# First stage of a streaming encoder step: other PSUM tiles for the first products and the token sums

## The chip, the cores and the metric

One core of a Trainium2 chip runs the whole program. The metric is the device time of one execution in microseconds (us); of several runs the median is given. The engines are PE (TensorE; PEld is its weight load), DVE (VectorE), ACT (ScalarE), POOL (GpSimd) and SP (SyncE, which here only issues DMAs).

## The reference, cut to what matters

One trunk layer is computed for 1024 prompt tokens and 32 sample tokens, with D = 1024. Only its beginning matters here: an RMS normalisation whose scale and shift come from a small matrix product with the condition `c`, and then one wide input projection, of which the first column blocks are keys, values and queries of the attention.

```
mod = silu(c) @ w_ada + b_ada
sh1, sc1, ... = split(mod)
h = rmsnorm(x, g_mix) * (1 + sc1) + sh1
u = h @ w_in
qa, ka, va, qm, km, vm, om, ip, fp, ga, gm = split(u)
# then: chunk-band attention on qa, ka, va; an mLSTM on qm..fp; merge gates ga, gm;
# output projection and residual; SwiGLU FFN and residual; final RMSNorm
```

## The kernel before

The 1024 + 32 tokens stand in the free dimension, in three token tiles of 352 columns (`TILES`); the first two are called early, the third late. The 1024 model channels stand in eight groups of 128 partitions (`k` = 0 to 7). Every product is made in three passes (`PASSES`), since weights and activations are each split into a high and a low part: high weight with high activation, low weight with high activation, high weight with low activation. A projection block is 128 columns of `w_in`; one block over one token tile takes 8 x 3 = 24 matmuls of 128x352.

`first_units` is the first stage. It makes the scales and shifts (`ada_sums` on PE, `ada_done` on ACT), the sums of squares of each token (`token_sums` on PE, read by DVE in `token_roots`), and then the products of three blocks at once: K, V and Q of the first pair of heads. For the two early tiles it goes through `k` = 0 to 7 and makes six matmuls in each pass (`products`); meanwhile ACT, DVE and POOL make the next `h` (`scaled_x`, `high_h`, `low_h`). At `k` = 3 PE makes the token sums of the late tile, POOL takes the roots, and at `k` = 4 PE spreads them (transposes on L543) and ACT copies them out (L544). `late_h` then makes the late tile's `h`. After the early products ACT and DVE take their results out of PSUM (`put_k`, `put_v`, `put_q`, lines 601 to 606, 642, 702 to 706). PE's next work is the late tile of K and V: 48 matmuls of line 475, `k` by `k`, K and V in turn, into the two places called `last`. The late tile of Q follows as an ordinary `unit` (line 402), into whose run the transposes of V (`v_tail`, L674; its results are taken out by ACT L662 and DVE L665) and of its sample rows (`v_sample`, L623 and L625) are put. Then come the next projection blocks, and with the second head pair's blocks the attention of the first (scores in a tile of `ps_s`, transposes in `ps_t`, values in `ps_v`).

PSUM has eight banks here: three tiles of one bank (`mm`), one tile `psS` of two banks, one tile `psT` of two banks (called `psA` in `first_units`), one tile `psV` of one bank (called `psH`). `tok` is the second half of a tile of two banks.

The order of the instructions of PE, ACT, DVE and POOL is the order of the code (`manual_schedule`); each of these engines works through its own list in that order. The waits between engines are put in by the framework, from which instruction writes or reads which tile.

## Time and profile before

| | |
|---|---|
| median of 3 runs | 1601.08 us (1599.99 to 1601.38) |
| the profiled execution | 1600.62 us, of which its span 1598.9 us |
| PE busy | 1569.6 us, 98% of the span |
| DVE, ACT, POOL busy | 1104.7, 793.8, 418.0 us |
| mean granted TensorE clock | 0.996 |

The span runs from the first to the last instruction of the profiled execution; 1.7 us of its time lie outside. Times in the views below are us from the start of the span. Matmuls overlap: one of 352 columns is listed with some 0.32 us, while the next starts 0.16 us after it. In a list of waits the engine that waited stands on the left and what it waited for on the right of the arrow. Tile names come without their numbers, and `s` stands for many tiles.

### The profile page before, as it was taken

The page shows a single profiled execution, that of the slowest core. Times are in us where ns is not written, and L with a number is a line of the kernel's source. Part 1 is how long each engine was busy: PE and PEld are TensorE (multiplying, and loading weights), DVE is VectorE, ACT ScalarE, POOL GpSimd, SP SyncE. Part 2 cuts the span into 40 slices and gives each one's busy share as a digit, 9 for nine tenths or more (in the row PEclk, how much of TensorE's full clock was granted, in tenths as well). Part 3 has the DMA queues.
Part 4 walks back from the last instruction along what each step waited for, and adds up shares of the span by engine and source line. Part 5 has one row for each costly group of instructions (what it writes and reads, how often), then busy time and mean ns, then how long its engine had stood idle before and what let it go on. Part 6 is the DMA issues. An engine that isn't in the chain of part 4 may idle for free.

```text
span 1598.9 us, 27295 instructions
## 1 busy us (share of the span) xinstructions
PE 1569.6 (98%) x10197; PEld 1552.4 (97%) x10197; DVE 1104.7 (69%) x2276; ACT 793.8 (50%) x1748; POOL 418.0 (26%) x439
## 2 busy tenths in 40 slices
PE   8899999999999999999999999999999999999997
PEld 8889999999999999999999999999999999999997
DVE  3656565556676845456654699988898886799755
ACT  4666454544555644444443655554544444545443
POOL 0324233433232411000012100566565650000000
PEclk9999999999999999999999999999999999999999
DMA  9222323242232332575353311313222227427444
GB/s 375 84 65 84 107 76 116 82 130 93 67 87 74 83 90 75 121 259 187 122 153 114 107 55 44 103 54 107 81 78 96 67 77 249 145 80 240 138 136 155
DMA packets 176329, 186.02 MB, mean 116 GB/s; under 512 B 11746, under 2 KB 141446, under 8 KB 176198
## 3 DMA queue, kind: packets, MB, share of 16 engines
q1 hardware_dynamic: 173542, 182.45, 36.1%
q10 hardware_dynamic: 2656, 1.83, 0.4%
q8 instruction: 80, 1.31, 0.3%
q14 instruction: 51, 0.42, 0.1%
HBM read 150.10 MB, written 34.16 MB: 115 GB/s over the span
## 4 chain that ended last, share of the span: by engine, by line
PE 90%; ACT 4%; DVE 3%; DMA 2%; issue 1%; POOL 0%; ACTq 0%; SPq 0%; DVEq 0%; POOLq 0%
PE mm L402 40%; PE psb L1869 18%; PE mm L1869 10%; PE psb L2251 3%; PE mm L946 3%; PE mm L2251 2%; PE psV L851 2%; PE psb L2115 2%; PE psS L792 1%; PE psT L819 1%; PE mm L2115 1%; DMA s<-in_w_ada_dram 1%; DMA s<-in_x_dram 1%; PE psV L1180 1%; PE psT L1182 1%
## 5 line engine op out<-in xcount | busy, mean ns | idle before, releaser
L402 PE MATMUL mm<-s,wsp 128*128 128x352 f32 x4104 | 687.0, 324 | 0.0
L402 PEld LDWEIGHTS mm<-s,wsp 128*128 128x128 f32 x4104 | 657.3, 188 | 1.8 <-issue 0.4
L365 DVE TENSOR_TENSOR wsp<-wraw,wsp 128x512 fp32r<-128x512 f32 (+1 forms) x280 | 235.9, 860 | 118.7 <-ACT wsp L364 116.7
L1869 PE MATMUL psb<-s,wsp 128*128 128x352 f32 x1611 | 271.7, 322 | 1.6 <-DVE wsp L365 0.9
L364 ACT ACTIVATE wsp<-wraw 128x512 fp32r<-128x512 f32 x336 | 199.6, 617 | 143.9 <-PE psb L1869 43.0
L1869 PEld LDWEIGHTS psb<-s,wsp 128*128 128x128 f32 x1611 | 260.6, 188 | 2.1 <-DVE wsp L365 1.1
L1869 PE MATMUL mm<-s,wsp 128*128 128x352 f32 x933 | 159.3, 322 | 0.0
L1869 PEld LDWEIGHTS mm<-s,wsp 128*128 128x128 f32 x933 | 151.2, 188 | 0.4 <-DVE wsp L365 0.4
L812 POOL TENSOR_SCALAR st<-st,mx 128x640 f32<-128x640 f32 (+5 forms) x72 | 53.2, 739 | 187.1 <-DVE mx L811 165.0
L1275 DVE CUSTOM_DVE_ANT_0 junk<-wa,t 128x512 bf16<-128x512 f32 x128 | 93.6, 731 | 1.1
L365 POOL TENSOR_TENSOR wsp<-wraw,wsp 128x512 fp32r<-128x512 f32 x56 | 74.7, 1354 | 56.8 <-ACT wsp L364 50.5
L806 DVE CUSTOM_DVE_ANT_0 st<-psS,bias 128x640 f32<-128x640 f32 (+5 forms) x72 | 44.5, 617 | 57.3 <-PE psS L792 42.5
L807 ACT ACTIVATE st<-st,mx 128x640 f32<-128x640 f32 (+5 forms) x72 | 47.9, 666 | 63.5 <-DVE mx L806 62.4
L1816 POOL TENSOR_TENSOR t<-t,sl 128x352 f32<-128x352 f32 x19 | 18.4, 968 | 212.7 <-ACT sl L1814 212.7
L826 ACT ACTIVATE pT<-psT 128x640 fp32r<-128x640 f32 (+3 forms) x80 | 38.5, 492 | 61.8 <-PE psT L819 49.3
L2224 POOL TENSOR_TENSOR fst<-fst,mhalf 128x6 f32<-128x6 f32 x1 | 2.3, 2311 | 221.1 <-DVE fst L2223 221.1
L831 DVE TENSOR_TENSOR pT<-psT,pT 128x640 fp32r<-128x640 f32 (+3 forms) x80 | 44.0, 558 | 22.5 <-ACT pT L826 22.4
L1488 POOL TENSOR_TENSOR wraw<-wraw,raw 128x512 f32<-128x512 f32 x33 | 55.8, 1704 | 0.9
L946 PE MATMUL mm<-s,s 128*128 128x264 f32 (+3 forms) x432 | 54.5, 283 | 0.0
L2251 PE MATMUL psb<-s,wsp 128*128 128x352 f32 x330 | 54.2, 324 | 0.0
L2251 PEld LDWEIGHTS psb<-s,wsp 128*128 128x128 f32 x330 | 53.1, 188 | 0.1
L946 PEld LDWEIGHTS mm<-s,s 128*128 128x128 f32 (+1 forms) x432 | 51.9, 179 | 0.5
(377 smaller groups left out, 2480.1 us busy)
## 6 DMA issues: line engine op xcount, KB each, us to landing
wraw<-in_w_in_dram SPq DMA_DIRECT2D x37, 512.0 KB, 3.6
wraw<-in_w_gate_up_dram SPq DMA_DIRECT2D x33, 512.0 KB, 4.0
wa<-in_w_mod_dram SPq DMA_DIRECT2D x64, 256.0 KB, 2.6
wraw<-in_w_down_dram SPq DMA_DIRECT2D x32, 512.0 KB, 4.5
a_d<-t SPq DMA_DIRECT2D x22, 528.0 KB, 2.6
g_d<-t SPq DMA_DIRECT2D x16, 528.0 KB, 3.0
t<-g_d SPq DMA_DIRECT2D x16, 528.0 KB, 4.6
s<-in_w_ada_dram SPq DMA_DIRECT2D x16, 512.0 KB, 8.6
```

The lines of the kernel that those rows point to most:

```text
L364: act.activation(dst[:, 0], src, AF.Copy)
L365: eng.tensor_tensor(dst[:, 1], src, f(dst[:, 0]), op=ALU.subtract)
L402: pe.matmul(pt[:, :hi - lo], wt[(w0 + k) // 4][:, a, (w0 + k) % 4], xt[k][:, b, lo:hi], start=(k == 0 and q == 0), stop=(k == n - 1 and q ...
L806: dve.tensor_tensor_reduce(so, sv, bi, -1.0, 3.0e38, ALU.add, ALU.min, mx[:n, 1:2])
L807: act.activation(st[:n, :w], st[:n, :w], AF.Exp, bias=mx[:n, 1:2], scale=-1.0, accum_out=mx[:n, 2:3])
L812: pool.tensor_scalar(st[:n, :w], st[:n, :w], mx[:n, 3:4], 1.0, op0=ALU.mult, op1=ALU.mult)
L946: pe.matmul(pt[:n, :wd], hs[k][:, a, i * P:i * P + n], whl[b][:, k, :wd], start=(k == 0 and q == 0), stop=(k == KD - 1 and q == 2))
L1275: dve.tensor_tensor_reduce(junk, wa, crow[:, c], 1.0, 0.0, ALU.mult, ALU.add, at)
L1488: self.eng.tensor_tensor(a(dst), a(x), a(y), op=op)
L1869: pe.matmul(acc, wt[:, a, k], x[k][:, b], start=(start and not onto and k == 0 and q == 0), stop=(stop and k == 3 and q == 2), skip_group_ ...
L2115: pe.matmul(acc, wt[k // 4][:, u, k % 4], piece_of[k, i][:, v], start=(k == 0 and q == 0), stop=(k == KP - 1 and q == 2))
L2251: pe.matmul(acc, wt[(k - k0) // 4][:, u, (k - k0) % 4], piece_of[k, 2][:, v], start=(k == 0 and q == 0), stop=(k == NF - 1 and q == 2))
```

## The change

It gives other tiles to the same instructions; no instruction is added, removed or moved. The token sums go from the second half of `psA` to that of `psS`; the sums for channel group 7 from `psH` to the first half of `psS`. V's two early tiles go from `psS` to `psA`, Q's from the first half of `psA` and an `mm` tile to an `mm` tile and `psH`. The late tiles of K and V go from `tok` (in `psA`) and `psH` to the two halves of `psS`.

```
-    tok = psA[:, 512:]
+    tok = psS[:, 512:]
...
-        pts = [[mmt(), mmt()], [psS[:, :512], psS[:, 512:]], [psA[:, :512], mmt()]]
-        last = [tok, psH]
+        pts = [[mmt(), mmt()], [psA[:, :512], psA[:, 512:]], [mmt(), psH]]
+        last = [psS[:, :512], tok]
...
-        ada_sums(7, 0, psH)
-        ada_sums(7, 1, psH)
+        ada_sums(7, 0, psS)
+        ada_sums(7, 1, psS)
...
-        ada_done(7, psH)
+        ada_done(7, psS)
```

The waits that the framework puts in change with the tiles. In the rows below `mm_363` and `mm_364` hold K, `s_347` to `s_550` are `h` of `k` = 0 to 7, and a wait names the engine waited for.

PE at `k` = 3, the token sums of the late tile and the third pass behind them, before:

```order
L304 MATMUL psT_150<-ones,t_153 128x32 [waits DVE_49]
L304 MATMUL psT_150<-ones,t_153 128x32
L304 MATMUL psT_150<-ones,t_153 96x32
L475 MATMUL mm_363<-s_422,wsp_327 128x352
L475 MATMUL mm_364<-s_422,wsp_327 128x352
L475 MATMUL psS_152<-s_422,wsp_330 128x352 x2
L475 MATMUL psT_150<-s_422,s_345 128x352 [waits DVE_49]
L475 MATMUL mm_365<-s_422,s_345 128x352
```

and after:

```order
L304 MATMUL psS_152<-ones,t_153 128x32 [waits DVE_49]
L304 MATMUL psS_152<-ones,t_153 128x32
L304 MATMUL psS_152<-ones,t_153 96x32
L475 MATMUL mm_363<-s_422,wsp_327 128x352
L475 MATMUL mm_364<-s_422,wsp_327 128x352
L475 MATMUL psT_150<-s_422,wsp_330 128x352 x2
L475 MATMUL mm_365<-s_422,s_345 128x352
L475 MATMUL psV_151<-s_422,s_345 128x352
```

The matmul of Q behind the sums waited for DVE, which reads the sums in the other half of its tile; it now has no wait.

PE where the early products end and the late tile of K and V begins, before (Q's early results are in `psT_150` and `mm_365`):

```order
L475 MATMUL psT_150<-s_550,s_345 128x352
L475 MATMUL mm_365<-s_550,s_345 128x352
L475 MATMUL psT_150<-s_347,wsp_327 128x352 [waits Activation_49]
L475 MATMUL psV_151<-s_347,wsp_330 128x352
L475 MATMUL psT_150<-s_347,wsp_327 128x352
L475 MATMUL psV_151<-s_347,wsp_330 128x352
L475 MATMUL psT_150<-s_347,wsp_327 128x352 [waits Pool_49]
L475 MATMUL psV_151<-s_347,wsp_330 128x352
L475 MATMUL psT_150<-s_390,wsp_327 128x352
```

and after:

```order
L475 MATMUL mm_365<-s_550,s_345 128x352
L475 MATMUL psV_151<-s_550,s_345 128x352
L475 MATMUL psS_152<-s_347,wsp_327 128x352 [waits Activation_49]
L475 MATMUL psS_152<-s_347,wsp_330 128x352
L475 MATMUL psS_152<-s_347,wsp_327 128x352
L475 MATMUL psS_152<-s_347,wsp_330 128x352
L475 MATMUL psS_152<-s_347,wsp_327 128x352 [waits Pool_49]
L475 MATMUL psS_152<-s_347,wsp_330 128x352
L475 MATMUL psS_152<-s_390,wsp_327 128x352 [waits Activation_49]
```

K and V of the late tile now stand in one tile, and each `k` has a wait for ACT of its own, where one wait on the first matmul covered all of them.

ACT where the late tiles of K and V are taken out (L601 and L604 read K, L642 reads V), before:

```order
L364 ACTIVATE wsp_741<-wraw_497 128x512 [waits PE_49]
L601 ACTIVATE s_657<-psT_150 64x352 [waits PE_49]
L601 ACTIVATE s_657<-psT_150 64x352
L604 ACTIVATE kf_658<-psT_150 128x352
L642 ACTIVATE t_668<-psV_151 128x352 [waits PE_49]
L662 ACTIVATE s_766<-mm_767 128x8x64 [waits PE_49]
```

and after:

```order
L364 ACTIVATE wsp_741<-wraw_497 128x512 [waits PE_49]
L601 ACTIVATE s_657<-psS_152 64x352 [waits PE_49]
L601 ACTIVATE s_657<-psS_152 64x352
L604 ACTIVATE kf_658<-psS_152 128x352
L642 ACTIVATE t_668<-psS_152 128x352 [waits DVE_49]
L662 ACTIVATE s_766<-mm_767 128x8x64 [waits PE_49]
```

ACT's read of V's late tile now waits for DVE, whose two reads of K's late tile (L606) are in the same tile.

## The prediction

> **What bounds the kernel now.** I read the page's first and fourth part, then the chain of waits in order of time, then PE's own waits from 24 to 84 us, and last the timeline around each of them.

> ```profile
> PE 1569.6 (98%) x10197; PEld 1552.4 (97%) x10197; DVE 1104.7 (69%) x2276; ACT 793.8 (50%) x1748; POOL 418.0 (26%) x439
> PE 90%; ACT 4%; DVE 3%; DMA 2%; issue 1%; POOL 0%; ACTq 0%; SPq 0%; DVEq 0%; POOLq 0%
> ```

> PE is busy nearly throughout and carries 90% of the chain that ended last, so a microsecond in which PE stands still in the first stage is, as far as this goes, a microsecond of the whole. PE's waits in the stage that the change touches are these:

> ```profile
> PE psT L475 <- ACT s L704: 3.7, 1, 3.7
> PE psT L475 <- DVE roots L315: 1.1, 1, 1.1
> ```

> Both are matmuls on `psT`, held up by a reader of the same tile's other contents. The longer one stands between the early products and the late tile:

> ```profile
> 64.40 1.86 ACT L601 ACTIVATE s<-mm 64x352 fp32r<-64x352 f32 x4
> 64.48 0.32 PE L475 MATMUL mm<-s,s 128*128 128x352 f32 x1
> 64.57 0.25 POOL L356 TENSOR_TENSOR s<-s,s 128x32 fp32r<-128x32 f32 x1 [0.77 <-ACT s L348]
> 67.53 0.95 ACT L704 ACTIVATE s<-psT 64x352 fp32r<-64x352 f32 x2
> 68.53 0.66 PE L475 MATMUL psT<-s,wsp 128*128 128x352 f32 x1 [3.73 <-ACT s L704]
> 68.86 0.93 ACT L704 ACTIVATE s<-mm 64x352 fp32r<-64x352 f32 x2
> 78.84 1.61 PE L402 MATMUL mm<-s,s 128*128 128x352 f32 x9
> ```

> PE starts its last early product at 64.48 and stands until ACT has taken Q out of `psT` (67.53 + 0.95). And it comes back slow, as the granted clock (the number behind POOL's in each row) and the chain show:

> ```profile
> 67.00:68.00 1.00, 0.00 (x0) 0.00 (x0) 0.68 (x2) 0.99 (x3) 0.00 (x0) 0.63 0.00 0
> 68.00:74.00 6.00, 5.47 (x19) 5.47 (x20) 2.57 (x4) 1.72 (x4) 2.72 (x4) 0.50 0.00 0
> 74.00:75.00 1.00, 1.00 (x8) 1.00 (x8) 0.00 (x0) 0.00 (x0) 0.00 (x0) 0.96 0.00 0
> 73.68 0.49 PE L475 MATMUL psV<-s,wsp 128*128 128x352 f32 x1
> 73.59 0.29 PE psT L475
> 77.56 0.16 PE psV L475
> ```

> A mean of 0.63 between 67 and 68 means full speed for 0.26 us and half after it: the clock fell at 67.26 and came back at 74.08 (0.96 in the last row: half for 0.08 us). Matmuls follow each other at 0.29 us in that time, at 0.16 outside it.

> **The change, part by part.** All sums are against the profiled execution, 1600.62 us with 1598.9 of span; the median of the runs, 1601.08, lies 0.46 above it.

> *The late tile of K and V.* With no wait the next matmul would start at 64.48 + 0.16 = 64.64. The wait for Q goes, because `psS` holds nothing but token sums and scales by then, both read before 56 us. What is left to wait for is `h` of the late tile: its last piece is POOL's row at 64.57, done at 64.82, and it belongs to `k` = 7, some 7 us later in PE's list; the waits for ACT at each `k` are for that same `h`. So 48 matmuls take 48 x 0.16 = 7.68 us, where before PE needed 78.84 - 64.64 = 14.20 (3.89 of standing, 10.31 of work, of which 2.63 is the half clock). Gain 6.52 us. Between bounds: 3.89 if the clock fell all the same, 6.52 if not; nothing is left that would make PE stand, so I take the upper one.

> *The token sums at `k` = 3 and the spread roots at `k` = 4.*

> ```profile
> 50.62 0.49 PE L475 MATMUL psS<-s,wsp 128*128 128x352 f32 x2
> 52.00 0.15 DVE L315 TENSOR_SCALAR roots<-psT 96x1 f32<-96x1 f32 x1
> 52.20 0.43 PE L475 MATMUL psT<-s,s 128*128 128x352 f32 x1 [1.09 <-DVE roots L315]
> 52.23 1.49 POOL L316 TENSOR_TENSOR roots<-roots,mhalf 128x3 f32<-128x3 f32 x1 [19.27 <-DVE roots L315]
> 52.47 0.33 PE L475 MATMUL mm<-s,s 128*128 128x352 f32 x1
> 54.54 0.47 PE L543 MATMUL psT<-ident,roots 128*128 128x128 f32 x3
> 55.04 0.47 ACT L544 ACTIVATE t<-psT 128x352 f32<-128x352 f32 x1 [1.12 <-PE psT L543]
> 55.19 0.49 PE L475 MATMUL psS<-s,wsp 128*128 128x352 f32 x2
> 55.56 0.43 PE L475 MATMUL psT<-s,s 128*128 128x352 f32 x1
> 55.83 0.32 PE L475 MATMUL mm<-s,s 128*128 128x352 f32 x1
> ```

> Without the wait, the matmul at 52.20 would start at 50.62 + 2 x 0.16 = 50.94 and the one at 52.47 at 51.10: 1.37 us. But DVE's reads stay where they are (DVE works without a break there), and so does POOL's power, done at 53.72, which the transposes need. PE would come to them at 54.54 - 1.37 = 53.17 and now waits: 53.72, 0.05 for the signal (52.15 to 52.20 at the first wait) and some 0.16 for the weight load ahead of it (an estimate: the spacing of two matmuls) give 53.93. So 0.61 of the 1.37 is left, and the new stop is POOL. Then the wait for ACT's copy goes: the matmul at 55.83 would have started at 55.19 + 3 x 0.16 = 55.67, so 0.16 more. Gain 0.77; bounds 0.16 (POOL's end later than listed) and 1.53.

> *ACT's new wait.* K's and V's late results are now one tile. Before, L642 read V beside DVE's reads of K:

> ```profile
> 80.17 0.46 ACT L642 ACTIVATE t<-psV 128x352 f32<-128x352 f32 x1
> 80.31 1.06 DVE L606 TENSOR_TENSOR s<-psT,s 64x352 fp32r<-64x352 f32 x2 [9.61 <-ACT kf L604]
> 80.92 0.60 ACT L662 ACTIVATE s<-mm 128x512 fp32r<-128x512 f32 x1 [0.28 <-PE mm L674]
> 81.68 0.60 PE L674 MATMUL mm<-ident,t 128*128 128x128 f32 x4
> 82.32 0.60 ACT L662 ACTIVATE s<-mm 128x512 fp32r<-128x512 f32 x1 [0.80 <-PE mm L674]
> 82.95 0.69 DVE L665 TENSOR_TENSOR s<-mm,s 128x512 fp32r<-128x512 f32 x1 [0.64 <-ACT s L662]
> 83.55 0.27 DVE L625 COPY stg<-mm 32x128 f32<-32x128 f32 x1
> 83.88 0.59 PE L402 MATMUL mm<-s,wsp 128*128 128x352 f32 x2
> ```

> In these times, L642 moves from 80.17 to 81.37 + 0.05 = 81.42 and ends at 81.88. Queued behind it on ACT are both L662, then a copy with its DMA and Q's L702. The second of the four transposes at 81.68 is the first that reads V's late columns, so PE stands about 0.3 us there; the second L662 goes from 82.32 to about 82.65; DVE's L665 and L625 follow it, and PE's next block waits for L625 at 83.88 already. Cost 0.35; bounds 0 (if ACT need not wait) and 1.25 (all that L642 moves). I take 0.35, by the row of L662, which has 0.80 of idle ahead of it to give.

> *What moves for nothing.* The split of the next weights (ACT L364, POOL L365) now comes before PE's end of the late tile, not in the middle of it:

> ```profile
> 68.08 2.96 POOL L706 TENSOR_SCALAR s<-s 64x352 fp32r<-64x352 f32 x4 [1.23 <-ACT s L704]
> 75.03 1.15 ACT L364 ACTIVATE wsp<-wraw 128x512 fp32r<-128x512 f32 x2 [5.24 <-PE psT L475]
> 75.80 2.54 POOL L365 TENSOR_TENSOR wsp<-wraw,wsp 128x512 fp32r<-128x512 f32 x2 [4.76 <-issue]
> 89.75 0.33 PE L792 MATMUL psS<-s,s 128*128 128x128 f32 x2
> 93.43 0.50 PE L792 MATMUL psS<-s,s 128*128 128x256 f32 x2 [1.35 <-DVE mx L806]
> ```

> ACT is free of Q at 68.86 + 0.93 = 69.79 and splits until 70.94; POOL is free at 71.04 and ends at 73.6. PE uses these weights at 83.88 - 7.29 + 0.35 = 76.94: 3.3 us of cover, and if it went, PE would stand for what POOL is late. The attention's first scores (89.75) need `psS` back, now from V's late read (about 74.6 on the new clock) and not from V's early one; they come at 82.8, so 8 us cover that. PE's wait at 93.43 ends a chain that starts from Q's late tile, which moves along; I leave it as it is.

> **Sum:** 6.52 + 0.77 - 0.35 = 6.94 us. 1600.62 - 6.94 = 1593.68 for an execution like the profiled one, 1594.14 from the median; I say 1594.0.

> **The rivals.** Clear of noise is about 0.2%, 3.2 us.

> *The half clock was not in every run (or comes again elsewhere).* PE stood 3.73 us, the clock fell 2.46 us after the last matmul's listed end at 64.80. If this is near an edge, most runs before may have kept the full clock; then only 6.94 - 2.63 = 4.31 us are won, 1596.8. Against it: the three timed runs lie between 1599.99 and 1601.38 around the profiled 1600.62, and none is 2.6 us below it. 0.07. [...]

> *The gain is given back later.* Something paced by other engines (the wait at 93.43, the chain's 4% of ACT and 3% of DVE) could hold its time while PE comes earlier. For it to eat 4 of 6.9 us, a chain would have to be fixed in time, not in the order; DMA, which alone is, has 2% of the chain. 1599, within 0.2%. 0.04.

> *The change does not do what it says:* the first late matmul's wait for ACT could still be for Q's copies. Against it: each later `k` has a wait for ACT of its own, and those instructions stand ahead of Q's copies in ACT's list, so the first wait is earlier still. About 0.8 - 0.35 would be left, 1600.6. 0.02.

> *Two blocks in turn in one tile.* If PE had to let each matmul land before the next one writes the tile's other half, the 48 would follow each other at the 0.32 us that one is listed with: 7.7 us more, 1601.4. If the gaps let the clock fall too, it is the 0.49 of the row at 73.68: 48 x 0.33 = 15.8 more, 1609.5. It is slower by over 0.2% from 0.16 + (6.94 + 3.2) / 48 = 0.37 us apiece on. Against it: the row at 50.62 has two matmuls into the two halves of `psS` in 0.49 us, which is 0.16 apart. 0.03.

> **How the numbers follow.** My forecast holds 0.84. Its own bounds are 1600.62 - (6.52 + 1.53 - 0) = 1592.6 and, with 0.16 for the token sums and 1.25 for ACT's wait, 1601.08 - 5.43 = 1595.7. The range goes a little past both, for the run-to-run 0.7 us, and up to the first rival's edge: 1592.3 to 1596.8. Faster holds the forecast and the first rival, 0.91; within 0.2% 0.06; slower 0.03.

> **What would show it.** In the new profile PE's waits for ACT L704 and DVE L315 are gone; the granted clock is 1.00 from 62 to 78 us; PE's first L402 starts near 71.5; PE stands some 0.7 us at L543 for POOL; ACT's L642 waits about 1 us for DVE L606; the first L792 comes near 82.8 and everything behind it some 6.9 us earlier, up to a span near 1592. If L402 starts late, the first term is wrong; if it starts at 71.5 and the span does not follow, the cover of a later stage was gone.

## The result, and the profile after

| | before | after |
|---|---|---|
| median | 1601.2 us | 1596.86 us (10 runs, 1596.02 to 1598.06) |
| ratio, 95% interval | | 0.9973 [0.9963, 0.9983] |
| the profiled execution | 1600.62 us | 1598.06 us, its span 1596.3 |
| mean granted clock in it | 0.996 | 0.997 |

The change gains 4.3 us where 6.94 were forecast; the median lies 2.9 us above the forecast and just past the upper end of its range. The profiled execution is the slowest of the ten. Its first loads come later as well: the matmul listed at 35.95 us in the trace of before stands at 36.71, which the following comparisons take off where they say so. Three slow runs of some thousand us (5479.48 of before, 5848.70 of e1, 6770.47 of after_again) are left out of all ranges and ratios; the medians hold them, and would be at most 0.24 us lower without.

The page's busy times and the shares of the chain:

```profile
PE 1568.8 (98%) x10197; PEld 1551.1 (97%) x10197; DVE 1105.4 (69%) x2276; ACT 796.2 (50%) x1748; POOL 421.4 (26%) x439
PE 88%; ACT 3%; DVE 3%; DMA 3%; issue 2%; POOL 0%; SPq 0%; ACTq 0%; DVEq 0%; POOLq 0%
```

PE's waits from 24 to 125 us (what waited, for what, us in total, times, longest):

```profile
PE mm L674 <- ACT t L642: 1.8, 1, 1.8
PE psV L851 <- ACT pT L826: 1.7, 1, 1.7
PE psS L792 <- DVE mx L806: 1.4, 1, 1.4
...
PE psS L543 <- POOL roots L316: 0.5, 1, 0.5
```

PE's waits for ACT L704 and DVE L315 are gone. At L543 the forecast stop for POOL is there. At the head stands a wait that the prediction had put at about 0.3 us. The timeline of PE around the late tile of K and V, and then of ACT and DVE behind it:

```profile
54.58 0.52 PE L543 MATMUL psS<-ident,roots 128*128 128x128 f32 x3 [0.45 <-POOL roots L316]
64.59 7.84 PE L475 MATMUL psS<-s,wsp 128*128 128x352 f32 x48
72.27 1.61 PE L402 MATMUL mm<-s,s 128*128 128x352 f32 x9
75.11 0.27 PE L674 MATMUL mm<-ident,t 128*128 128x128 f32 x1
77.16 0.55 PE L674 MATMUL mm<-ident,t 128*128 128x128 f32 x3 [1.78 <-ACT t L642]
79.31 6.02 PE L402 MATMUL mm<-s,wsp 128*128 128x352 f32 x36
```

```profile
67.49 1.87 ACT L601 ACTIVATE s<-mm 64x352 fp32r<-64x352 f32 x4
72.93 1.16 ACT L364 ACTIVATE wsp<-wraw 128x512 fp32r<-128x512 f32 x2
74.11 0.93 ACT L601 ACTIVATE s<-psS 64x352 fp32r<-64x352 f32 x2
75.55 1.06 DVE L606 TENSOR_TENSOR s<-psS,s 64x352 fp32r<-64x352 f32 x2 [1.73 <-ACT kf L604]
76.64 0.47 ACT L642 ACTIVATE t<-psS 128x352 f32<-128x352 f32 x1 [1.12 <-DVE s L606]
```

All 48 matmuls run through at full speed in 7.68 us (64.59 to 72.27; the row's 7.84 goes to the listed end of the last), and the first L402 comes at 72.27 instead of 78.84. But ACT takes K's early tiles out from 67.49 on (64.40 before), comes to K's late tile at 74.11, 1.8 us after PE has gone on to L402, and V's read, L642, follows at 76.64. PE's second set of transposes has waited 1.78 us for it. So one question is why ACT is 3.1 us later than before, 2.3 beside the start.

A second loss stands further on. The table by stretches (us; PE, PEld, DVE, ACT and POOL busy; granted clock; DMA share; GB/s):

```profile
101.00:104.00 3.00, 1.63 (x11) 1.10 (x9) 1.06 (x3) 2.94 (x5) 0.42 (x1) 1.00 0.20 81
104.00:105.00 1.00, 0.33 (x1) 0.36 (x2) 0.97 (x3) 0.60 (x2) 0.39 (x1) 0.85 0.00 0
105.00:108.00 3.00, 3.00 (x12) 3.00 (x12) 1.65 (x6) 0.92 (x2) 0.80 (x1) 0.50 0.00 0
108.00:109.00 1.00, 1.00 (x7) 1.00 (x7) 0.00 (x0) 0.22 (x1) 0.00 (x1) 0.95 0.00 0
```

Around the stop at L851 the clock fell from 104.70 to 108.11. PE's lead over the trace of before shrinks by 1.54 us there: at L851 it is 109.21 - 104.67 = 4.54 us, at the next L819 112.54 - 109.54 = 3.00.

### The profile page after: what moved, and what is told of

Read it like the earlier page. It is cut to its first block, busy times and chain, and to the rows that moved or that the text cites. A ratio compares the mean times of both kernels' runs of the same rounds, so it can differ in the third digit from the quotient of the medians.

```text
span 1596.3 us, 27296 instructions
## 1 busy us (share of the span) xinstructions
PE 1568.8 (98%) x10197; PEld 1551.1 (97%) x10197; DVE 1105.4 (69%) x2276; ACT 796.2 (50%) x1748; POOL 421.4 (26%) x439
## 4 chain that ended last, share of the span: by engine, by line
PE 88%; ACT 3%; DVE 3%; DMA 3%; issue 2%; POOL 0%; SPq 0%; ACTq 0%; DVEq 0%; POOLq 0%
PE mm L402 38%; PE psb L1869 18%; PE mm L1869 11%; PE psb L2251 3%; PE mm L946 3%; PE mm L2251 2%; PE psV L851 2%; PE psb L2115 2%; PE psS L792 1%; PE psT L819 1%; PE mm L2115 1%; DMA s<-in_w_ada_dram 1%; DMA s<-in_x_dram 1%; PE psV L1180 1%; PE psT L1182 1%
## 5 line engine op out<-in xcount | busy, mean ns | idle before, releaser
L402 PE MATMUL mm<-s,wsp 128*128 128x352 f32 x4104 | 688.6, 324 | 0.1
L402 PEld LDWEIGHTS mm<-s,wsp 128*128 128x128 f32 x4104 | 658.7, 189 | 2.2 <-issue 0.4
L365 DVE TENSOR_TENSOR wsp<-wraw,wsp 128x512 fp32r<-128x512 f32 (+1 forms) x280 | 236.8, 863 | 118.5 <-ACT wsp L364 115.7
L364 ACT ACTIVATE wsp<-wraw 128x512 fp32r<-128x512 f32 x336 | 200.0, 618 | 139.0 <-PE psb L1869 41.5
L365 POOL TENSOR_TENSOR wsp<-wraw,wsp 128x512 fp32r<-128x512 f32 x56 | 74.1, 1344 | 52.0 <-ACT wsp L364 50.5
L806 DVE CUSTOM_DVE_ANT_0 st<-psS,bias 128x640 f32<-128x640 f32 (+5 forms) x72 | 44.5, 618 | 58.7 <-PE psS L792 44.0
L826 ACT ACTIVATE pT<-psT 128x640 fp32r<-128x640 f32 (+3 forms) x80 | 38.6, 494 | 61.6 <-PE psT L819 49.1
```

What stands on the lines that cost most here:

```text
L364: act.activation(dst[:, 0], src, AF.Copy)
L365: eng.tensor_tensor(dst[:, 1], src, f(dst[:, 0]), op=ALU.subtract)
L402: pe.matmul(pt[:, :hi - lo], wt[(w0 + k) // 4][:, a, (w0 + k) % 4], xt[k][:, b, lo:hi], start=(k == 0 and q == 0), stop=(k == n - 1 and q ...
L806: dve.tensor_tensor_reduce(so, sv, bi, -1.0, 3.0e38, ALU.add, ALU.min, mx[:n, 1:2])
```

## Why ACT is late: what the two traces say

POOL makes the late tile's sample columns at L337, right after ACT's L544. The timelines of POOL and ACT, before:

```profile
55.58 1.18 POOL L337 TENSOR_TENSOR s<-s,t 128x32 f32<-128x32 f32 x3 [1.87 <-ACT t L544]
56.69 0.40 ACT L347 ACTIVATE s<-s,sh,s 128x32 f32<-128x32 f32 x1
```

and after:

```profile
55.68 4.44 POOL L337 TENSOR_TENSOR s<-s,t 128x32 f32<-128x32 f32 x3 [1.15 <-ACT t L544]
59.73 0.42 ACT L347 ACTIVATE s<-s,sh,s 128x32 f32<-128x32 f32 x1 [2.26 <-POOL s L337]
```

Three operations on 128x32 took 1.18 us before and 4.44 after, the first alone 4.02. DVE in the same stretch, after:

```profile
55.46 0.95 DVE L354 SCALAR_TENSOR_TENSOR s<-s,sh,s 128x704 fp32r<-128x704 f32 x1
56.32 1.48 DVE L335 SCALAR_TENSOR_TENSOR s<-s,s,t 128x320 f32<-128x320 f32 x3
57.71 1.41 DVE L354 SCALAR_TENSOR_TENSOR s<-s,sh,s 128x320 fp32r<-128x320 f32 x2
59.03 0.55 DVE L335 SCALAR_TENSOR_TENSOR s<-s,s,t 128x320 f32<-128x320 f32 x1
60.90 0.55 DVE L354 SCALAR_TENSOR_TENSOR s<-s,sh,s 128x320 fp32r<-128x320 f32 x1 [1.32 <-ACT s L345]
```

DVE ran L335 and L354 without a break until 59.58, and POOL's first operation ended at 59.70. ACT waited 2.26 us for POOL.

My theory at this point was that the earlier roots bring POOL to its turn inside DVE's stream, where it is kept out, and that this costs PE 1.8 us, with 1.4 more from the clock. The rival was that ACT's new wait behind DVE L606 is simply dearer than I had said.

## The experiments

Each edit stands against the changed kernel. Runs of one job share a chip and its runs of the kernel before; those had medians of 1601.57 (e1 to e4), 1601.03 (after_again, e5 to e7) and 1601.33 us (the rest).

**e1: V's late tile is taken out ahead of K's.**

```
-        W.advance()
+        W.advance(); put_v(*late, last[1][:, :NT]); first[id(W.blocks[1])] = [None] * 3
```

> The changed kernel with V's late tile taken out before K's, so that ACT's L642 has no wait for DVE's L606. Theory 1 (ACT's new wait, met by an ACT that is late already, costs 1.78 us of PE at L674): L642 comes right behind the weight split, near 73.0 + 1.1 = 74.1 us, and ends before V's second transposes want it at 75.2; PE's wait for L642 falls from 1.78 to under 0.3 us; 1.4 to 1.8 us faster than the changed kernel. Rival (the lateness of ACT decides, not its order): K's copies, now behind L642, and the two L662 behind them hold PE as long at the next block (L402 behind L625): under 0.5 us.

1596.54 us (1594.0 to 1597.22), 0.9964 [0.9953, 0.9976]. In its profile PE's second set of transposes has no gap:

```profile
75.00 0.60 PE L674 MATMUL mm<-ident,t 128*128 128x128 f32 x4
```

I first read this as V's order having cured the wait. It could not tell: in this execution POOL's first L337 took 0.84 us, not 4.02, so ACT was not late at all. The clock fell at 424.87 instead, behind another stop, which the kernel had before as well (PE's waits from 410 to 432 us):

```profile
PE psT L819 <- DVE pT L831: 2.0, 1, 2.0
```

This execution took 1596.06 us; what the other runs of e1 met is not seen.

**e2: the sample columns of L337 are made on DVE.**

```
-                pool.tensor_tensor(x, x, RB[:, a:b], op=ALU.mult)
+                dve.tensor_tensor(x, x, RB[:, a:b], op=ALU.mult)
```

> The changed kernel with the late tile's 32 sample columns multiplied by DVE in place of POOL (eight operations of 128x32, L337). Theory 2 (POOL's first L337 took 4.02 us, where it took 0.25 before, because DVE ran on without a gap from 55.5 to 59.6 us; ACT's late h waited 2.26 us for it): ACT's first L347 comes near 57.4 in place of 59.73, ACT ends the copies of Q some 2.3 us earlier and is ready when PE ends the late tile; PE's wait for L642 falls from 1.78 to about 0.3 us, as in the prediction; 1.3 to 1.7 us faster than the changed kernel. Rival (ACT is late for another reason, for example its own reads of PSUM beside a running PE): ACT's L601 for K's early tile stays near 67.5 and the time stays within 0.4 us.

1596.22 us (1594.69 to 1596.48), 0.9966 [0.9953, 0.9978]. The wait for L642 went, but the next POOL operation was shut out, longer still (POOL's timeline):

```profile
57.94 7.50 POOL L356 TENSOR_TENSOR s<-s,s 128x32 fp32r<-128x32 f32 x1 [3.58 <-ACT s L348]
```

DVE went on with its L335, L337 and L354 until 65.3. PE had to wait 0.27 us for that operation inside the late tile. And the clock fell at 425.29. The median gains 0.6 us on the changed kernel's first one, not the 1.3 to 1.7 that I expected.

**e3: the late tile's first L335 goes one place earlier on DVE, so that DVE itself waits for L544 there.**

```
-            if 0 <= k < KD:
+            if 1 <= k < KD:
                 scaled_x(k, *late)
...
-                scaled_x(k + 2, 0, CUT)
+                scaled_x(k + 2, 0, CUT); k == 5 and scaled_x(0, *late)
```

> The changed kernel with one DVE operation moved: the first late L335, which has to wait for ACT's L544, stands one place earlier, ahead of an L354, so that DVE stands still for a moment when POOL's first L337 asks. Same operations on the same engines. Theory 2 in its narrow form (POOL gets in only where DVE has a gap): POOL's first three L337 take about 1.2 us together, as before the change, not 4.44, and the gain is that of the kernel with the sample columns on DVE, 1.3 to 1.7 us. Rival (the sum of DVE's work decides, not the gap): the first L337 still takes over 2 us and the time stays within 0.4 us.

1594.66 us (1594.34 to 1594.95), 0.9958 [0.9945, 0.997]: 6.9 us below before, what the prediction had summed (the repeat further down gives 5.8). POOL gets in at once: the first L337 takes 0.25 us, as before the change, though DVE's L335, which the same L544 released, had started 0.04 us ahead of it. And PE's transposes have no stop of note (timelines of POOL and PE):

```profile
55.83 1.58 POOL L337 TENSOR_TENSOR s<-s,t 128x32 f32<-128x32 f32 x3 [1.15 <-ACT t L544]
75.26 0.95 PE L674 MATMUL mm<-ident,t 128*128 128x128 f32 x4
```

**e4: ACT's side work before the attention starts four steps earlier,** to take the stop at L851 away.

```
-            ada = side.start(ada_rest(), ADA_STEPS, 495)
+            ada = side.start(ada_rest(), ADA_STEPS, 495); [side.step(ada) for _ in range(4)]
```

> The changed kernel with the first Silu of the condition rows (ACT L1269) some 18 us earlier, before the first Exp, which saves ACT two table loads of 1.28 us near 98 and 101 us and so the stall of PE at 103 us (1.73 us, L851 waiting for L826). Theory 3 (this stall lets PE's clock fall for one window of 3.41 us in about half of the executions, which costs 1.4 us there, and splits the runs into 1596.1 and 1597.4): the profile has no half clock between 95 and 115 us, all timed runs lie in one group with the higher mean clock, and the time is 1.5 to 3 us below the changed kernel's. Rival (the clock falls there at random, whatever PE does): the runs still fall into two groups 1.3 us apart.

1595.49 us (1593.78 to 1595.84), 0.996 [0.9946, 0.9974]. The stop did not go away, it moved (PE's waits):

```profile
PE psS L792 <- DVE mx L806: 2.5, 1, 2.5
PE mm L674 <- ACT t L642: 1.7, 1, 1.7
...
PE psV L851 <- ACT pT L826: 0.2, 1, 0.2
```

There is no half clock between 95 and 115 us, as expected, but it now fell behind L792, at 89.54. The median is 1.4 us below the changed kernel's first, where I expected 1.5 to 3. POOL was kept out in this execution (4.44 us for the first three L337), and the wait for L642 stands beside it. The edit also shortened the stop at L819 near 424 us, from 2.0 to 0.84 us, which I had not foreseen.

**after_again and after_third: the changed kernel itself, two more times.**

> The changed kernel once more. Theory 3 (PE's clock falls for 3.41 us at the end of a clock window in which PE stood over about 1.9 us; where the windows lie is another in each execution): in the trace the clock's edges have another phase than before (104.70 and 108.11 us there), and a fall comes only after a window with 2.0 us or more of standing PE; runs between 1596.0 and 1598.1. Theory 2: POOL's first L337 takes 4 us again and PE waits 1.8 us for L642. Rival (both were chance of one execution): POOL's first L337 takes 0.25 us, no wait for L642.

> The changed kernel once more, unedited, to count. Theory (two lots, each drawn anew in every execution): POOL's first operation at L337 takes either about 0.84 us or about 4.0 us, and the granted clock falls for one window of 3.41 us or not. The four levels are then about 1594.2 (neither), 1595.6 (the clock alone), 1596.1 (POOL alone) and 1597.5 us (both), and the runs stand on them; in the profile PE waits 1.5 us or more for ACT L642 if L337 took over 3 us, and under 0.3 us if it took under 1 us. Rival (ACT's new wait for DVE costs this much by itself): PE waits 1.5 us or more for L642 in the profile, however long L337 takes.

Medians of 1597.47 us (eight runs from 1594.16 to 1598.73), 0.9975 [0.9965, 0.9986], and 1595.84 (5 runs, 1594.27 to 1596.45), 0.9964 [0.9952, 0.9977]. Both profiles show an execution some 4 us shorter than the first, with no more than the forecast 0.3 us at L642 and no fall of the clock. The timelines of POOL and ACT, then of PE, in the one of 1594.16 us:

```profile
55.40 1.77 POOL L337 TENSOR_TENSOR s<-s,t 128x32 f32<-128x32 f32 x3 [1.15 <-ACT t L544]
57.09 0.40 ACT L347 ACTIVATE s<-s,sh,s 128x32 f32<-128x32 f32 x1
64.80 1.87 ACT L601 ACTIVATE s<-mm 64x352 fp32r<-64x352 f32 x4
72.22 0.93 ACT L601 ACTIVATE s<-psS 64x352 fp32r<-64x352 f32 x2 [0.84 <-PE psS L475]
74.76 0.46 ACT L642 ACTIVATE t<-psS 128x352 f32<-128x352 f32 x1 [1.13 <-DVE s L606]
```

```profile
72.03 1.61 PE L402 MATMUL mm<-s,s 128*128 128x352 f32 x9
74.87 0.95 PE L674 MATMUL mm<-ident,t 128*128 128x128 f32 x4
77.42 6.05 PE L402 MATMUL mm<-s,wsp 128*128 128x352 f32 x36
```

and the same stretch as above by the clock:

```profile
101.00:104.00 3.00, 1.26 (x10) 1.29 (x10) 2.41 (x8) 1.64 (x6) 0.80 (x1) 1.00 0.00 0
105.00:108.00 3.00, 3.00 (x23) 2.98 (x22) 0.57 (x2) 1.17 (x2) 0.80 (x1) 1.00 0.00 0
```

ACT waits for PE at L601 here, not PE for ACT. L642 waits for DVE just as long (1.13 and 1.12 us), so that wait is not what differs: the rival falls. The stop at L851 is the same too, and the clock stays.

So one kernel has two lots in it, two things that fall out anew in each execution: whether POOL is kept out, and whether the clock falls. Between the two traces of it, PE's L674 differs by 77.16 - 75.27 = 1.89 us, of which 72.27 - 72.03 = 0.24 was there before: being kept out costs 1.65. The clock's fall adds 1.54: the first trace is 104.67 - 102.74 = 1.93 us behind the other at L851 and 109.54 - 106.07 = 3.47 us at the next L819. The clock has a second place to fall, the stop of 2.00 us at L819 near 424 us; it did so in the profiles of e1, e2 and e8. The 23 runs of the changed kernel stand in groups: four at 1594.2 to 1594.7, nine at 1595.8 to 1596.5, nine at 1597.3 to 1598.1 and one at 1598.73. That fits neither, one, both, and one fall more; only the three profiled ones (1594.16, 1594.27 and 1598.06) are seen, so the rest is a reading.

**e5: the part with the token sums alone.** The late tile of K and V waits for Q's place again.

```
-        last = [psS[:, :512], tok]
+        last = [pts[2][0], psS[:, :512]]
```

> The changed kernel, but the late tile of K goes into Q's first mm tile, so that PE waits again until ACT has taken Q out: the token sums' part of the change alone. The prediction's sum for this part: 0.77 us faster than before, 1600.4 to 1600.8. Theory 2 (the earlier copy L544 meets DVE in mid-stream, POOL's L337 takes 4 us, ACT's late h and with it Q's copies end some 2.3 us later): PE stands until near 71.6 us instead of 68.5 and the kernel is slower than before, by 1.5 to 3 us, 1603 to 1604.5.

1602.21 us (11 runs), 1.0009 [1.0, 1.0018]: seven runs at 1600.5 to 1602.3 and four at 1603.4 to 1603.9. The profiled one, the slowest, is of the upper group, and POOL was kept out in it, which PE's wait for Q shows in full (POOL's timeline, then PE's waits):

```profile
55.72 4.44 POOL L337 TENSOR_TENSOR s<-s,t 128x32 f32<-128x32 f32 x3 [1.15 <-ACT t L544]
```

```profile
PE mm L475 <- ACT s L704: 6.8, 1, 6.8
```

**e8: e5 with e3's edit.**

> Token sums and roots in their new tiles, the late tile of K and V still in the old ones (as in e5), and the first late L335 one place earlier on DVE (as in e3). Theory (the token part is worth 0.7 us, and e5 lost it since POOL was kept out at L337): L337 takes under 1 us, PE comes back at L475 within 0.5 us of before and not 3.1 later, about 1600.4 us, the runs within 1.5 us of each other. Rival (the token part costs time by itself, through the later chain of ACT): about 1602.2 us, like e5.

1601.85 us (11 runs, 1600.76 to 1602.24), 1.0003 [0.9994, 1.0012]. The same two views:

```profile
56.02 1.58 POOL L337 TENSOR_TENSOR s<-s,t 128x32 f32<-128x32 f32 x3 [1.15 <-ACT t L544]
```

```profile
PE mm L475 <- ACT s L704: 4.4, 1, 4.4
```

The upper group is gone: no run over 1602.24. But the gain of 0.7 us that I expected is not there. PE's wait for Q has grown from 3.7 to 4.4 us; its end is set by ACT's reads of Q, which come hardly earlier. Beside the start of each trace PE comes to this wait 0.83 us ahead of before and leaves it 0.16 ahead, so most of the token part is lost in it. The first L402 is 1.12 us ahead, since the clock was halved for one window of 3.41 us here and for two before, and another fall at 431.33, behind L819, takes more than that back. So the token part alone shows no gain in the medians, and where POOL is kept out (e5's profile) PE leaves the wait 2.3 us later than before, beside the start. I had e5 and e8 apart by 1.8 us; their medians are 0.4 apart, since only four of e5's eleven runs stand in its upper group.

**e6 and e7: e3 with e1, and with e1 and e4.**

> The kernel with one DVE operation moved (POOL gets its gap) and V taken out before K (no wait of L642 for DVE). With ACT on time, L642's wait is worth what the prediction said, 0.35 us: 1594.3, 0.2 to 0.5 us below the kernel with the gap alone (1594.66), about what can be told. Rival (the wait is worth 1.8 us wherever ACT stands): 1592.9.

> All three: DVE's gap for POOL, V before K, and the early Silu that spares two table loads. Theory 3: PE's wait at L851 near 103 us falls from 1.7 to 0.2 us, that at L792 near 88 us grows by up to 1.1 us since ACT does the Silu ahead of it; 0.5 to 1.5 us below the kernel without the Silu edit, near 1593.2, if no window takes 2 us of standing at L792, and 1.4 more in executions where one does. Rival (table loads were hidden): no difference.

> e3 once more, unedited. Theory (the moved L335 takes away POOL's lot): L337 takes under 1 us, no wait of PE for L642 of 0.3 us or more, 1594.3 to 1595.0 us, a run with the clock's fall up to 1596.0, none above. Rival (e3's five runs were luck of the same draw): runs at 1596.1 and 1597.5 us among them, as in the changed kernel.

> e7 once more, beside e3 on the same chip. Theory: 1593.2 to 1593.9 us, some 1 us below e3, since PE's stop at L851 goes from 1.7 to 0.2 us and the one at L792 grows from 1.4 to 2.5 us, where the clock falls for a window in some executions. Rival (it differs from e3 by the clock's draw alone): the two medians within 0.3 us.

e6: 1595.83 us (1593.88 to 1596.96), 0.9965 [0.9952, 0.9978], 1.5 above what I expected; the second L674 group takes 0.60 us as in e1, and the clock fell at L851, at 103.40. e3 again: 1595.57 us (1594.21 to 1596.58), 0.9964 [0.9951, 0.9976], with two runs above the 1596.0 that I had set as the most. Its profiled run, of 1594.21, has no fall and POOL in at once, so the clock is likely in the other three, but not seen. e7: 1593.65 us (1593.17 to 1593.82), 0.9954 [0.9941, 0.9967], and again 1593.49 (1593.25 to 1593.63), 0.9952 [0.9938, 0.9965]. It is the best version: 3.3 us below the changed kernel's first median, 2.1 below e3 on the same chip, and its ten runs lie within 0.65 us. In both profiles its clock falls once, behind the one stop of 2.5 us at L792, and nowhere else until PE's work ends. By my expectation such a fall adds 1.4 us to 1593.2, and the times do not show it; the same edit also cuts the stop at L819 near 424 us from 2.0 to 0.8 us, which I had not counted. With L851's stop at 0.2 us and L819's at 0.8 the clock fell at neither in the two profiles. The spread fits that; whether the clock fell in the eight runs that were not profiled is not seen, and a version with one of the parts alone was not timed beside it.

## Why the prediction was right or wrong, point by point

*The late tile (6.52 us): right.* No wait, full clock, 48 matmuls in the 7.68 us that were forecast; PE's first L402 comes 72.27 - 78.84 - 0.76 = 7.33 us earlier beside the later start, and 6.52 + 0.77 = 7.29 had been said.

*Token sums and roots (0.77 us): right here, but bound to the first term.* L543 comes 0.72 us earlier beside the start, with 0.45 of waiting for POOL where 0.7 were forecast, and the last early product comes 0.82 earlier. e8 shows that most of this is lost again in the wait for Q as long as the late tile has that wait.

*ACT's new wait (0.35 us): the step that failed.* Its mechanism and size are right where ACT is on time: in after_again L674's second group takes 0.95 us instead of 0.60, which is 0.35, and V's read first takes it away (e1). What failed is "ACT is free of Q at 68.86 + 0.93 = 69.79" and the late `h` "done at 64.82", both taken over from before although the second term moves the spread roots (L543 and ACT's L544), and with them POOL's start at L337, by 0.6 us. In the first profile ACT comes free of Q at 72.93 by L364's start, 2.4 us later than that beside the later start, and the term is 0.35 + 1.65 = 2.0 us, outside its bounds of 0 to 1.25. POOL's order against DVE had not been looked at.

*The sum.* In the execution where POOL was let in and the clock stayed, the next block's first L402 comes at 77.42: 83.88 - 77.42 + 0.49 for that trace's later start (36.44 us for the matmul at 35.95) is 6.95 us, against 6.94 forecast, and the time is 1594.16. So the sum held for that case, and e3, which takes POOL's lot away, had medians of 1594.66 and 1595.57. Against 1593.68 the first profile's 1598.06 has 0.76 from its start, 1.61 from POOL (79.31 is 5.33 us earlier, not 6.94), 1.54 from the clock and 0.5 in the rest of the program, which I did not trace.

*The rivals.* None came as written. The half clock was there before, as the profile of before shows, and did not return at the late tile (a mean of 1.00 from 62 to 78 us in the first profile); but "comes again elsewhere" did happen, at a stop that the kernel had before as well, and I had given that no price of its own. That is the second step that failed: the sum is taken against one trace, in which PE stood 1.74 us at L851 and 2.00 us at L819 and kept its full clock, and lets every execution do so. It cost 1.54 us in the first profile. That the median lies near this rival's 1596.8 is luck. Only one execution of before was profiled, so how often its clock falls at these two stops, and how much of the gap between forecast and median is the clock's, stays open. The gain was not given back at the wait of L792. The tiles did what was said, and two blocks in turn in one tile cost nothing (0.16 us apart).

*Behind POOL's row.* Why the first L337 takes 0.84 or 4.02 us in the same kernel is not settled: DVE's stream is as unbroken in the one as in the other, and the starts of its instructions against POOL's agree within some 10 ns. What the traces show is where such an operation ended: the 0.84 us of after_again 0.12 us behind the listed end of the one L354 that was under way (56.24 against 55.18 + 0.94 = 56.12), the 4.02 us of after 0.12 us behind that of a run of seven instructions of DVE (59.70 against 59.58), and the 7.50 us of e2's L356 0.11 us behind that of DVE's last L354 (65.44 against 63.86 + 1.47 = 65.33). In the last two POOL was passed over at more than one change of instruction on DVE. And in before (55.54 and 55.58 us) and in the six profiles with e3's edit POOL's operation took 0.25 us although a DVE L335 had started 0.04 us ahead of it.

## What to carry to other kernels

When a change makes one engine's small operation earlier, look at whose stream it now falls into: here a 128x32 operation on POOL was shut out by DVE for 4 or 7.5 us, and a place where DVE itself waits for the same signal let it in each time (0.25 us in six profiles of six). A term priced with "that engine is free by then" needs that engine's own inputs moved by the other terms first. And where a kernel's runs fall into groups, profile it more than once before explaining a median: here a single profile showed the slowest case, and the one that matched the forecast was the same program.
